# A recurrent layer's scans and factors placed behind its last convolution, and weights prepared three products ahead

## The chip, the cores and the metric

The kernel runs on one core of one Trainium2 chip. A core has five engines that work side by side, each with a queue of its own that it works off in order: TensorE (PE: matrix products, with its weight loads shown as PEld), VectorE (DVE: elementwise work and scans), ScalarE (ACT: functions from tables, copies), GpSimd (POOL: elementwise work, DMA issue) and SyncE (SP: DMA issue). They wait for each other by semaphores. The metric is the device time of one execution in microseconds (us), the median of several runs.

## The reference

A two-layer encoder in float32 on 512 tokens of width 1024. Layer 0 mixes tokens with a stick-breaking attention, layer 1 with a gated linear recurrence; behind each mixer stands an MLP with a squared ReLU (inner width 4096). What matters here, cut:

```python
def rglru_block(h, ...):
    proj = h @ w_in                                   # 1024 -> 2 * 1024
    gate = gelu(proj[..., :1024])
    xc = causal_depthwise_conv(proj[..., 1024:], conv_w, conv_b)    # 4 taps
    r = sigmoid(blocks(xc) @ w_a + b_a)               # 16 blocks of 64 x 64
    i = sigmoid(blocks(xc) @ w_x + b_x)
    log_a = -8 * r * softplus(-lam)
    a = exp(log_a)
    bterm = sqrt(-expm1(2 * log_a)) * (i * xc)
    hs = scan(a, bterm)                               # h[t] = a[t] * h[t-1] + b[t]
    return (hs * gate) @ w_o

def squared_relu_mlp(h, w1, w2):
    u = relu(h @ w1)
    return (u * u) @ w2
```

The last operation is an RMS norm of the sum.

## The kernel before

**Products.** Activations lie with 128 channels on the partitions and the 512 tokens along the row, so 1024 channels are eight blocks, c = 0 to 7. A float32 product is made of three faster ones: each operand is cut into a high half (ScalarE's cast, `wh`, `bh`, `xgh`) and a low half, operand minus high half (VectorE's subtraction, `wl`, `bl`, `xgl`); `three` (L194 to L198) multiplies high by high, high by low, low by high. So each weight slab of 128 x 1024 goes through DMA (L178), a cast (L184) and a subtraction (L191; or on GpSimd, L187 and an accumulating DMA, L188) before TensorE can use it.

**The order of the work.** TensorE's order is the order of the program's text. The other engines' orders are set by a scheduler from priorities and its own estimate of times; `tc.issue_after(x)` makes it place an instruction behind instruction x in the queue. In the recurrent layer `after(x)` is the same.

**The recurrent layer** is a list of steps (L1148). `conv(c)` multiplies a slab of `w_in` (24 products of 128x512), scales by the norm (L1068), makes the convolution from one ScalarE operation (L1075) and three taps on VectorE (L1077), then the high half `bh` (L1083, ScalarE) and the low half `bl` (L1084, VectorE). `gates(c)` multiplies these by the 128x256 gate weights (L1097 to L1099, six products) and takes two sigmoids (L1104, L1105). `rates(chunks)` makes the factors: Tanh (L1113), Exp (L1115), and two VectorE operations (L1117, L1119) with one on GpSimd (L1118). `recur(chunks)` takes Sqrt (L1126), multiplies (L1127) and scans (L1130). `gate(c)` multiplies the other half of `w_in` and keeps it in `z` (L1136); `gated(chunks)` takes Gelu (L1141), multiplies with the scans' result (L1143) and cuts the product into halves (`bh` in L1144, `bl` in L1145), in the same `bh` and `bl` tiles: the operand of the output projection. Change of a function's table on ScalarE is an instruction of its own (ACT_TABLE_LOAD). The blocks go through factors, scans and gating in three groups: 0 to 2, 3 to 5, 6 and 7. Before the change the factors of the second group wait in ScalarE's queue for the high half of convolution 6 (`high` at that time), and its scans in VectorE's for the last tap (`tap`) of convolution 7.

**The output projection** (L1165) runs over the eight columns k of the gated operand, and for each over four output blocks with three products: 96 products, in the banks `ps_o` and `ps_z`.

**The MLP's second product** (`Mlp.down`) makes a quarter of the inner width at a time, as seven products P1 to P7 on sums of blocks instead of eight; each has two halves g. `block` adds two weight blocks (L861, or an accumulating DMA, L854), `operand` cuts them (L839 on ScalarE, L840 on VectorE), `times` multiplies (L873), `collect` adds a bank to the result `c` (L882). In the last quarter an explicit order stands: `prepare` sums and cuts the weights of a product two places ahead of the product. The collects of P2 come behind the cut of the latest prepared weights. In the last MLP, `end` squares, scales and stores the output tokens; `finish` scales two halves of a token block, one of them on VectorE (L1223).

Of the kernel before, what the change touches and what calls it, by code (L numbers as in the profile page):

```python
# [14 lines left out]
ALU = mybir.AluOpType  # L15
# [3 lines left out]
S = 512  # L19
# [28 lines left out]
def hybrid_encoder(  # L48
# [22 lines left out]
    V, A, G, PE = nc.vector, nc.scalar, nc.gpsimd, nc.tensor  # L71
# [195 lines left out]
    with ExitStack() as actx:  # L267
# [18 lines left out]
        for i in range(2):  # L286
            both = []
            for nm in ("h", "l"):
                t = sp.tile([P, 2 * P], F32R, tag=f"last{nm}{i}", name=f"last{nm}{i}")
# [434 lines left out]
    class Mlp:  # L724
# [118 lines left out]
        def block(self, q4, name, g, far):  # L843

            _, b, to, *_ = self.PRODUCTS[name]
            if b == "b21":
                t = wpool.tile([P, C, P], F32, tag="raw", name="raw", bufs=3)
                t = t.rearrange("p (j k) f -> p j (k f)", j=2)
                nc.sync.dma_start(out=t, in_=self.weights(q4, g, b))
                self.raws[b, g] = t  # L850
            raw = self.raws[b, g]
            if name in far:

                G.dma_start(out=raw, in_=self.weights(q4, g, to), accum_op=ALU.add)  # L854
            elif to:

                ahead = None
                if far and (name, g) != ("P5", 0):
                    ahead = self.ready if name == "P5" else self.before
                with tc.issue_after(ahead.ins) if ahead else nullcontext():  # L860
                    V.tensor_tensor(raw, raw, self.raws[to, g], ALU.add)  # L861
            return self.operand(raw)

        def times(self, name, g, i, w, ps, new, cols=slice(0, S)):
# [13 lines left out]
        def collect(self, name, i, ps, cols=slice(0, S)):  # L878
            out, less = self.PRODUCTS[name][4:]
            y = self.c[out][:, i, cols]  # L880
            if (out, i) in self.begun:
                V.tensor_tensor(y, y, ps, ALU.subtract if less else ALU.add)  # L882
            else:
                self.begun.add((out, i))
                A.activation(y, ps, AF.Copy, scale=-1.0 if less else 1.0)

        def down(self, q4, far=(), end=None):
            sums = {}

            def product(name, g, w=None):  # L890
                w = w or self.block(q4, name, g, far)
                to = self.PRODUCTS[name][3]
                new = name in ("P1", "P5", "P2")
                if to not in sums:
                    sums[to] = [self.bank() for _ in range(2)]
                for i in range(2):
                    self.times(name, g, i, w, sums[to][i], new)
                if g:

                    first = end and name == "P2"  # L900
                    with tc.issue_after(self.cut.ins) if first else nullcontext():
                        for i in range(2):
                            self.collect(name, i, sums[to][i])

            if end is None:
                for name in ("P1", "P5", "P6", "P3", "P7", "P2", "P4"):
                    for g in range(2):
                        product(name, g)
                return

            order = [("P1", 0), ("P5", 0), ("P2", 0), ("P1", 1), ("P2", 1), ("P5", 1)]
            order += [(name, g) for name in ("P6", "P3", "P7", "P4") for g in range(2)]
            ws = {}

            def prepare(*at):

                if at != ("P7", 1):
                    self.before = self.cut
                ws[at] = self.block(q4, *at, far)

            for at in order[:2]:
                prepare(*at)
            for at, ahead in zip(order[:-2], order[2:]):
                prepare(*ahead)
                product(*at, ws.pop(at))
            end([ws["P4", g] for g in range(2)], sums["X"])

# [83 lines left out]
    with ExitStack() as rctx:  # L1011
# [25 lines left out]
        def after(act):  # L1037

            return tc.issue_after(act.ins) if act is not None else nullcontext()

        xc, aa, om, z, hs, gin, gw, exps = ({} for _ in range(8))

        TURNS = ["acc", "acc", "t", "t", "o", *("acc", "acc", "t", "t") * 3]
        turns = [0, 0]
# [17 lines left out]

        def conv(c):

            nonlocal begin, tap, high, low
            ps = dense_in(C + c)
            with after(low if c < 3 else None):
                V.tensor_tensor(ps, ps, r, ALU.mult)  # L1068
            aa[c], xc[c], om[c] = (
                rp1.tile([P, S], F32, tag=t, name=t, bufs=n)  # L1070
                for t, n in (("aa", 5), ("bt", 6), ("om", C))
            )
            x0 = xc[c]
            taps = [cw[:, i * C + c : i * C + c + 1] for i in range(4)]
            begin = A.activation(x0, ps, AF.Identity, bias=col("conv_b")[:, c : c + 1], scale=taps[3])  # L1075
            for d in range(1, 4):
                tap = V.scalar_tensor_tensor(  # L1077
                    x0[:, d:], ps[:, : S - d], taps[3 - d], x0[:, d:], ALU.mult, ALU.add
                )

            i = C - 4 + c % 4
            xch, xcl = bh[:, i, :], bl[:, i, :]
            high = A.copy(xch, x0)  # L1083
            low = V.tensor_tensor(xcl, x0, f(xch), ALU.subtract)  # L1084
            gin[c] = xch, xcl
            if c < 3:
                gw[c] = gate_weights(c)
# [20 lines left out]
        def rates(chunks):  # L1108

            for c in chunks:  # L1110
                a0 = rp2.tile([P, S], F32, tag="a0", name="a0")
                with after(sig), after(high if c < 6 else None):
                    ex = A.activation(om[c], aa[c], AF.Tanh, scale=c4[:, c : c + 1])  # L1113
                with after(ex):
                    exps[c] = ex = A.activation(a0, aa[c], AF.Exp, scale=c8[:, c : c + 1])  # L1115
                d = rp2.tile([P, S], F32, tag="d", name="d")
                V.scalar_tensor_tensor(d, a0, 1.0, om[c], ALU.add, ALU.mult)  # L1117
                G.tensor_scalar(aa[c], d, -1.0, 1.0, ALU.mult, ALU.add)  # L1118
                V.scalar_tensor_tensor(xc[c], a0, 1.0, xc[c], ALU.add, ALU.mult)  # L1119

        def recur(chunks):
            nonlocal mark
            ex = exps[chunks[-1]]
            for c in chunks:
                with after(ex):
                    mark = A.activation(om[c], om[c], AF.Sqrt)  # L1126
                V.tensor_tensor(xc[c], xc[c], om[c], ALU.mult)  # L1127

                with after(low if c < 3 else tap if c < 6 else None):
                    V.tensor_tensor_scan(om[c], aa[c], xc[c], 0.0, ALU.mult, ALU.add)  # L1130
                hs[c] = om[c]

# [11 lines left out]
                A.copy(bh[:, c, :], z[c])  # L1144
                V.tensor_tensor(bl[:, c, :], z[c], f(bh[:, c, :]), ALU.subtract)  # L1145

        sig = begin = tap = high = low = None
        for what, c in (  # L1148
            (conv, 0), (conv, 1), (conv, 2), (gate, 0), (gate, 1), (gates, 0), (conv, 3), (gates, 1),
            (gate, 2), (gates, 2), (conv, 4), (gates, 3), (rates, range(3)), (conv, 5),  # L1150
            (recur, range(3)), (gates, 4), (gate, 3), (conv, 6), (gates, 5), (gate, 4),
            (rates, range(3, 6)), (conv, 7), (recur, range(3, 6)), (gates, 6), (gate, 5), (gated, range(6)),
            (gate, 6), (gates, 7), (rates, range(6, C)), (recur, range(6, C)), (gate, 7),
            (gated, range(6, C)),
        ):
            with tc.high_priority() if what is conv else nullcontext():
                what(c)
# [17 lines left out]
    with ExitStack() as mctx:  # L1175
# [35 lines left out]
            y = mlp.y(t, h)[:, cols]  # L1211
            G.tensor_tensor(y, y, gb[:, h * S : (h + 1) * S][:, cols], ALU.mult)

        def finish(t, h, i, cut=None):

            ts = slice(t * P, (t + 1) * P)
            rt = work.tile([P, 1], F32, tag="rt", name="rt")
            A.activation(rt, ss[:, t, i : i + 1], AF.Sqrt, bias=bias[:, t : t + 1], scale=1.0 / D)
            V.reciprocal(rt, rt)
            done, y = mlp.y(t, 1 - h), mlp.y(t, h)  # L1220
            A.activation(done, done, AF.Copy, scale=rt)
            nc.sync.dma_start(out=out[ts, (1 - h) * S : (2 - h) * S], in_=done)
            V.scalar_tensor_tensor(  # L1223
                y[:, cut:], y[:, cut:], rt, gb[:, h * S : (h + 1) * S][:, cut:], ALU.mult, ALU.mult
            )
            if cut:
                V.tensor_scalar(y[:, :cut], y[:, :cut], rt, None, ALU.mult)
            nc.sync.dma_start(out=out[ts, h * S : (h + 1) * S], in_=y)

        def end(ws, xs):  # L1230
            for t in range(2):
                square(t, 0, 0)
                scaled(t, 0)
                square(t, 1, 1, end=True)
                finish(t, 1, 1)
            for t in range(2, 4):
                square(t, 1, 0)
                scaled(t, 1)
# [83 lines left out]
```

## Time and profile before

| | us |
|---|---|
| median of 3 runs | 1083.57 (1082.63 to 1083.65) |
| the profiled execution | 1083.71 |
| its span, first to last instruction | 1082.0 |
| TensorE busy | 1061.5 |
| VectorE busy | 820.7 |
| ScalarE busy | 568.0 |
| GpSimd busy | 169.3 |

A row of a timeline has the start and the duration in us, the engine, the line of the kernel, the operation, output <- input by the program's names and shapes; in brackets the idle time of the engine before it, and what ended that. Equal instructions that follow each other are merged into one row with their count (x2). Consecutive instructions of an engine overlap by some 0.1 us, so a row's end is a little behind the next row's start. PE rows overlap by more: matmuls are pipelined, and their distance counts rather than their duration. A row of windows has a stretch, its length, the busy time and count of each engine, then the granted clock of TensorE as a share of its full speed (PEclk), the DMA share and GB/s.

### The profile page before, as it was taken

The page shows a single profiled execution, that of the slowest core. Times are in us where ns is not written, and L with a number is a line of the kernel's source. Part 1 is how long each engine was busy: PE and PEld are TensorE (multiplying, and loading weights), DVE is VectorE, ACT ScalarE, POOL GpSimd, SP SyncE. Part 2 cuts the span into 40 slices and gives each one's busy share as a digit, 9 for nine tenths or more (in the row PEclk, how much of TensorE's full clock was granted, in tenths as well). Part 3 has the DMA queues.
Part 4 walks back from the last instruction along what each step waited for, and adds up shares of the span by engine and source line. Part 5 has one row for each costly group of instructions (what it writes and reads, how often), then busy time and mean ns, then how long its engine had stood idle before and what let it go on. Part 6 is the DMA issues. An engine that isn't in the chain of part 4 may idle for free.

```text
span 1082.0 us, 13601 instructions
## 1 busy us (share of the span) xinstructions
PE 1061.5 (98%) x4992; PEld 879.0 (81%) x4992; DVE 820.7 (76%) x1073; ACT 568.0 (52%) x826; POOL 169.3 (16%) x199
## 2 busy tenths in 40 slices
PE   8999999999999999999999999899999999999997
PEld 6888888787888888888888777687888888888885
DVE  7788787829897597597687868975696597597776
ACT  6767676726554344344346467944445344344345
POOL 2344444410000000000001654022000000000012
PEclk9999999999999999999999999899999999999999
DMA  7745454526205305305342694242305305305103
GB/s 232 198 118 144 126 145 96 158 75 250 81 27 187 98 20 175 117 18 178 98 83 74 167 221 118 78 159 94 117 20 175 117 12 184 117 5 190 59 13 104
DMA packets 44034, 125.71 MB, mean 116 GB/s; under 512 B 7744, under 2 KB 8512, under 8 KB 43968
## 3 DMA queue, kind: packets, MB, share of 16 engines
q1 hardware_dynamic: 41088, 115.94, 34.3%
q0 software_dynamic: 2304, 8.39, 4.5%
q8 instruction: 39, 0.64, 0.2%
q10 hardware_dynamic: 576, 0.52, 0.2%
q14 instruction: 27, 0.22, 0.1%
HBM read 104.91 MB, written 2.10 MB: 99 GB/s over the span
## 4 chain that ended last, share of the span: by engine, by line
PE 82%; DVE 7%; ACT 5%; DMA 3%; issue 2%; SPq 0%; ACTq 0%; DVEq 0%
PE ps_t L873 9%; PE ps_o L873 6%; PE ps_z L873 6%; PE ps_acc L196 5%; PE ps_acc L197 5%; PE ps_acc L198 5%; PE ps_acc L873 5%; PE ps_o L196 4%; PE ps_o L198 4%; PE ps_o L197 4%; PE ps_z L196 3%; PE ps_z L197 3%; PE ps_t L196 3%; PE ps_z L198 3%; PE ps_t L197 3%; PE ps_t L198 3%
## 5 line engine op out<-in xcount | busy, mean ns | idle before, releaser
L184 ACT CAST wh<-raw 128x1024 fp32r<-128x1024 f32 (+2 forms) x136 | 119.8, 902 | 133.1 <-PE ps_o L198 34.5
L839 ACT CAST wh<-b 128x1024 fp32r<-128x1024 f32 x96 | 100.3, 1050 | 130.8 <-PE ps_o L873 25.0
L191 DVE TENSOR_TENSOR wl<-raw,wh 128x1024 fp32r<-128x1024 f32 (+2 forms) x126 | 132.2, 1065 | 25.8 <-ACT wh L184 25.7
L840 DVE TENSOR_TENSOR wl<-b,wh 128x1024 fp32r<-128x1024 f32 x96 | 116.9, 1222 | 24.3 <-ACT wh L839 24.2
L196 PE MATMUL ps_acc<-xgh,wh 128*128 128x512 f32 x304 | 122.4, 403 | 1.2 <-ACT wh L165 0.8
L197 PE MATMUL ps_acc<-xgh,wl 128*128 128x512 f32 x304 | 119.1, 392 | 0.5 <-DVE wl L166 0.5
L198 PE MATMUL ps_acc<-xgl,wh 128*128 128x512 f32 x304 | 119.0, 392 | 0.1
L854 POOL DMA_DIRECT2D b<-in_w_dn x6 | 5.4, 906 | 638.3 <-DVE wl L840 315.2
L548 DVE TENSOR_TENSOR_SCAN scan<-keep,later 128x128 f32<-128x128 f32 (+1 forms) x64 | 59.3, 927 | 19.8 <-ACT keep L538 15.6
L196 PE MATMUL ps_o<-xgh,wh 128*128 128x512 f32 x176 | 69.5, 395 | 0.2 <-DVE x L700 0.2
L197 PE MATMUL ps_o<-xgh,wl 128*128 128x512 f32 x176 | 68.6, 390 | 0.0
L198 PE MATMUL ps_o<-xgl,wh 128*128 128x512 f32 x176 | 68.6, 390 | 0.0
L198 PEld LDWEIGHTS ps_acc<-xgl,wh 128*128 128x128 f32 x304 | 57.1, 188 | 12.8 <-DVE xgl L116 0.5
L196 PE MATMUL ps_t<-xgh,wh 128*128 128x512 f32 x168 | 67.1, 399 | 0.0
L793 ACT ACTIVATE u<-u 128x512 f32<-128x512 f32 x64 | 39.4, 630 | 52.5 <-DVE u L792 52.5
L196 PEld LDWEIGHTS ps_acc<-xgh,wh 128*128 128x128 f32 x304 | 57.1, 188 | 11.6 <-ACT wh L165 1.0
L197 PE MATMUL ps_t<-xgh,wl 128*128 128x512 f32 x168 | 66.1, 393 | 0.0
L198 PE MATMUL ps_t<-xgl,wh 128*128 128x512 f32 x168 | 66.0, 393 | 0.0
L197 PEld LDWEIGHTS ps_acc<-xgh,wl 128*128 128x128 f32 x304 | 57.3, 188 | 10.5 <-DVE wl L166 1.2
L552 POOL TENSOR_TENSOR w<-w,scan 128x128 f32<-128x128 f32 (+1 forms) x64 | 53.7, 841 | 52.5 <-DVE scan L548 49.8
L861 DVE TENSOR_TENSOR b<-b,b 128x1024 f32<-128x1024 f32 x46 | 56.0, 1219 | 0.2
L803 DVE TENSOR_TENSOR u<-u 128x256 f32<-128x256 f32 x128 | 49.5, 420 | 2.4 <-ACT u L793 1.7
(325 smaller groups left out, 2745.7 us busy)
## 6 DMA issues: line engine op xcount, KB each, us to landing
raw<-in_w_m SPq DMA_DIRECT2D x64, 512.0 KB, 3.6
b<-in_w_dn SPq DMA_DIRECT2D x48, 512.0 KB, 4.2
raw<-in_w_dn SPq DMA_DIRECT2D x16, 512.0 KB, 3.5
raw<-in_w_in SPq DMA_DIRECT2D x16, 512.0 KB, 4.2
raw<-in_w_qk SPq DMA_DIRECT2D x12, 512.0 KB, 3.6
wl<-raw POOLq DMA_DIRECT2D x10, 512.0 KB, 6.0
x<-in_xT SPq DMA_DIRECT2D x16, 256.0 KB, 4.6
raw<-in_w_ro SPq DMA_DIRECT2D x8, 512.0 KB, 3.3
```

The source lines that it names most:

```text
L184: A.copy(wh[:, k, :], raw[:, k, :])
L191: V.tensor_tensor(wl[:, k, :], raw[:, k, :], f(wh[:, k, :]), ALU.subtract)
L196: PE.matmul(ps, wh, ah, start=start, stop=False)
L197: PE.matmul(ps, wl, ah, start=False, stop=False)
L198: PE.matmul(ps, wh, al, start=False, stop=stop)
L548: V.tensor_tensor_scan(sc[:, S - n : S][:, ::-1], keep[:, :n][:, ::-1], later[:, S - n :][:, ::-1], 1.0, ALU.mult, ALU.max,)
L552: G.tensor_tensor(wt, wt, sc[:, S - n + 1 : S + 1], ALU.mult)
L803: V.tensor_tensor(u[:, out, :], u[:, x, :], u[:, y, :], op)
L839: A.copy(wh, raw)
L840: self.cut = V.tensor_tensor(wl, raw, f(wh), ALU.subtract)
L861: V.tensor_tensor(raw, raw, self.raws[to, g], ALU.add)
L873: PE.matmul(ps, x[:, block, ts], y[:, jj, cols], start=first and n == 0, stop=last and n == 2, skip_group_check=not new,)
```

## The change

Four edits:

1. In the list of steps convolution 7 comes ahead of the second group's factors. Those factors now wait in ScalarE's queue for the high half of convolution 7 (a dictionary `highs` keeps each; the first group's still wait for convolution 4's, and the third's for none).
2. The second group's scans wait in VectorE's queue for convolution 7's low half instead of its last tap.
3. In the last quarter of both MLPs weights are prepared three products ahead instead of two. P2's collects come behind the latest sum of blocks (L861) instead of the latest cut, and P5's behind the last cut of P6's weights.
4. In the last MLP the VectorE scaling of the first two token blocks comes behind the latest collect (`mlp.added`).

The order of TensorE's and of SyncE's instructions is unchanged; on the other three queues instructions change places, and none is added or removed.

```diff
         def down(self, q4, far=(), end=None):
...
-                    first = end and name == "P2"
-                    with tc.issue_after(self.cut.ins) if first else nullcontext():
+                    first = {"P2": self.sum, "P5": last_cut.get("P6")}.get(name) if end else None
+                    with tc.issue_after(first.ins) if first else nullcontext():
                         for i in range(2):
                             self.collect(name, i, sums[to][i])
...
                 ws[at] = self.block(q4, *at, far)
-
-            for at in order[:2]:
+                last_cut[at[0]] = self.cut
+
+            for at in order[:3]:
                 prepare(*at)
-            for at, ahead in zip(order[:-2], order[2:]):
-                prepare(*ahead)
+            for at, ahead in zip(order[:-2], (*order[3:], None)):
+                if ahead:
+                    prepare(*ahead)
                 product(*at, ws.pop(at))
...
-            high = A.copy(xch, x0)
+            highs[c] = high = A.copy(xch, x0)
...
-                with after(sig), after(high if c < 6 else None):
+                with after(sig), after(highs.get(chunks[-1] + 2)):
                     ex = A.activation(om[c], aa[c], AF.Tanh, scale=c4[:, c : c + 1])
...
-                with after(low if c < 3 else tap if c < 6 else None):
+                with after(low if c < 6 else None):
                     V.tensor_tensor_scan(om[c], aa[c], xc[c], 0.0, ALU.mult, ALU.add)
...
-            (recur, range(3)), (gates, 4), (gate, 3), (conv, 6), (gates, 5), (gate, 4),
-            (rates, range(3, 6)), (conv, 7), (recur, range(3, 6)), (gates, 6), (gate, 5), (gated, range(6)),
+            (recur, range(3)), (gates, 4), (gate, 3), (conv, 6), (gates, 5), (gate, 4), (conv, 7),
+            (rates, range(3, 6)), (recur, range(3, 6)), (gates, 6), (gate, 5), (gated, range(6)),
...
-            V.scalar_tensor_tensor(
-                y[:, cut:], y[:, cut:], rt, gb[:, h * S : (h + 1) * S][:, cut:], ALU.mult, ALU.mult
-            )
+            with tc.issue_after(last.ins) if last else nullcontext():
+                V.scalar_tensor_tensor(
+                    y[:, cut:], y[:, cut:], rt, gb[:, h * S : (h + 1) * S][:, cut:],
+                    ALU.mult, ALU.mult,
+                )
...
-                finish(t, 1, 1)
+                finish(t, 1, 1, last=mlp.added)
```

More of the change, by code (lines that the diff above doesn't have):

```diff
@@ L860, in block @@
                 with tc.issue_after(ahead.ins) if ahead else nullcontext():
-                    V.tensor_tensor(raw, raw, self.raws[to, g], ALU.add)
+                    self.sum = V.tensor_tensor(raw, raw, self.raws[to, g], ALU.add)
             return self.operand(raw)
@@ L881, in collect @@
             if (out, i) in self.begun:
-                V.tensor_tensor(y, y, ps, ALU.subtract if less else ALU.add)
+                self.added = V.tensor_tensor(y, y, ps, ALU.subtract if less else ALU.add)
             else:
@@ L887, in down @@
         def down(self, q4, far=(), end=None):
-            sums = {}
+            sums, last_cut = {}, {}
             def product(name, g, w=None):
@@ L1039, in after @@
             return tc.issue_after(act.ins) if act is not None else nullcontext()
-        xc, aa, om, z, hs, gin, gw, exps = ({} for _ in range(8))
+        xc, aa, om, z, hs, gin, gw, exps, highs = ({} for _ in range(9))
         TURNS = ["acc", "acc", "t", "t", "o", *("acc", "acc", "t", "t") * 3]
@@ L1063, in conv @@
         def conv(c):
-            nonlocal begin, tap, high, low
+            nonlocal begin, high, low
             ps = dense_in(C + c)
@@ L1076, in conv @@
             for d in range(1, 4):
-                tap = V.scalar_tensor_tensor(
+                V.scalar_tensor_tensor(
                     x0[:, d:], ps[:, : S - d], taps[3 - d], x0[:, d:], ALU.mult, ALU.add
@@ L1145, in gated @@
                 V.tensor_tensor(bl[:, c, :], z[c], f(bh[:, c, :]), ALU.subtract)
-        sig = begin = tap = high = low = None
+        sig = begin = high = low = None
         for what, c in (
@@ L1212, in scaled, with finish @@
             G.tensor_tensor(y, y, gb[:, h * S : (h + 1) * S][:, cols], ALU.mult)
-        def finish(t, h, i, cut=None):
+        def finish(t, h, i, cut=None, last=None):
             ts = slice(t * P, (t + 1) * P)
@@ L1222, in finish @@
             nc.sync.dma_start(out=out[ts, (1 - h) * S : (2 - h) * S], in_=done)
-            V.scalar_tensor_tensor(
-                y[:, cut:], y[:, cut:], rt, gb[:, h * S : (h + 1) * S][:, cut:], ALU.mult, ALU.mult
-            )
+            with tc.issue_after(last.ins) if last else nullcontext():
+                V.scalar_tensor_tensor(
+                    y[:, cut:], y[:, cut:], rt, gb[:, h * S : (h + 1) * S][:, cut:],
+                    ALU.mult, ALU.mult,
+                )
             if cut:
```

## The prediction, made before the result was known

> **What bounds the kernel now.** I read the page first, then TensorE's waits, then the timelines around the longest one.
>
> ```profile
> span 1082.0 us, 13601 instructions
> PE 1061.5 (98%) x4992; PEld 879.0 (81%) x4992; DVE 820.7 (76%) x1073; ACT 568.0 (52%) x826; POOL 169.3 (16%) x199
> ```
>
> TensorE is busy for 98% of the span, so only its own waits and slow stretches can be won or lost. Its waits (engine, tile and line, who was waited for: total us, times, longest):
>
> ```profile
> PE ps_o L1099 <- DVE bl L1084: 4.1, 2, 3.7
> PE ps_t L873 <- DVE c L882: 1.2, 2, 0.9
> PE ps_t L873 <- DVE wl L840: 0.6, 2, 0.4
> ```
>
> The first holds the longest wait: the gate products of channel block 7 wait for the low half of the last convolution. The other two belong to the last quarters of the two MLPs. TensorE's timeline (start, us, instruction, idle time before it):
>
> ```profile
> 671.63 0.39 PE L198 MATMUL ps_t<-xgl,wh 128*128 128x512 f32 x1
> 683.95 0.39 PE L198 MATMUL ps_acc<-xgl,wh 128*128 128x512 f32 x1
> 685.16 0.39 PE L1098 MATMUL ps_o<-bh,gl 128*128 128x512 f32 x1
> 689.21 0.79 PE L1099 MATMUL ps_o<-bl,gh 128*128 128x512 f32 x1 [3.66 <-DVE bl L1084]
> 690.23 0.63 PE L1098 MATMUL ps_o<-bh,gl 128*128 128x512 f32 x1
> 690.65 0.63 PE L1099 MATMUL ps_o<-bl,gh 128*128 128x512 f32 x1
> 697.92 0.40 PE L196 MATMUL ps_o<-bh,wh 128*128 128x512 f32 x1
> 698.39 0.40 PE L198 MATMUL ps_o<-bl,wh 128*128 128x512 f32 x1
> ```
>
> The last convolution's own product ends at 671.63 + 0.39 = 672.02. The gate products stall until 689.21. The rows at 690.23 and 690.65, one step, stand 0.42 us apart, those at 697.92 and 698.39, two steps, 0.47, so 0.23 a step: after the stall TensorE runs at half rate. At 697.92 the out-projection loop begins, with column 0 of the gated output (`bh`, `bl`). The windows show the granted clock (PEclk, the column after the bracketed counts):
>
> ```profile
> 686.50:687.00 0.50, 0.00 (x0) 0.00 (x0) 0.50 (x1) 0.50 (x2) 0.00 (x0) 0.98 0.00 0
> 687.00:687.50 0.50, 0.00 (x0) 0.00 (x0) 0.50 (x2) 0.50 (x2) 0.00 (x0) 0.50 0.00 0
> 693.00:693.50 0.50, 0.50 (x2) 0.40 (x2) 0.50 (x1) 0.50 (x2) 0.00 (x0) 0.50 0.00 0
> 693.50:694.00 0.50, 0.50 (x3) 0.36 (x3) 0.50 (x2) 0.50 (x2) 0.00 (x0) 0.69 0.00 0
> ```
>
> The clock halves at about 687.0, 1.4 us into the idle time, and is whole again at about 693.8, 4.6 us after work resumed; the half-rate phase is 6.8 us long.
>
> **Part 1: the scans behind the last low half.** VectorE's timeline:
>
> ```profile
> 664.71 1.52 DVE L1077 SCALAR_TENSOR_TENSOR bt<-ps_acc,colt,bt 128x511 f32<-128x511 f32 x2
> 666.74 0.74 DVE L1077 SCALAR_TENSOR_TENSOR bt<-ps_acc,colt,bt 128x509 f32<-128x509 f32 x1
> 683.99 3.45 DVE L1130 TENSOR_TENSOR_SCAN om<-aa,bt 128x512 f32<-128x512 f32 x3
> 687.35 1.20 DVE L191 TENSOR_TENSOR wl<-raw,wh 128x1024 fp32r<-128x1024 f32 x1
> 688.47 0.69 DVE L1084 TENSOR_TENSOR bl<-bt,bh 128x512 fp32r<-128x512 f32 x1
> 696.55 0.69 DVE L1117 SCALAR_TENSOR_TENSOR d<-a,om 128x512 f32<-128x512 f32 x1 [0.84 <-ACT a L1115]
> 697.76 1.10 DVE L1145 TENSOR_TENSOR bl<-z,bh 128x512 fp32r<-128x512 f32 x1
> 709.48 1.29 DVE L1145 TENSOR_TENSOR bl<-z,bh 128x512 fp32r<-128x512 f32 x2
> ```
>
> Three scans and a slab's low half (683.99 to 688.5) stand ahead of the low half L1084. In the changed order the whole of convolution 7 comes ahead of the second group's factors on VectorE and ScalarE. From 672.02: ScalarE casts two out-projection slabs first; the second takes the weight buffer that this product frees, so it runs 672.05 to 673.1 (1.05, the cast row below). VectorE then cuts that slab (1.20; the next instruction starts at 674.25), does three taps (1.52 + 0.74, to 676.5); ScalarE's high half runs 676.6 to 677.2, the low half is there at 677.9. TensorE wants it at about 684.6 (683.95 and three steps of 0.23): no wait, 6.7 us to spare. Scans, gated products and the slab's cut together stay off the path here.
>
> **Part 2: the factors behind that convolution.** Here the cost arises, on ScalarE's queue, which is in order. The factors (Tanh, Exp), Sqrt, the sigmoids of gate 6, the six Gelus, the sigmoids of gate 7 and block 6's factors now all stand between 677.1 and the copy of column 0 (`bh`, L1144); before, the factors were done ahead of convolution 7 and the copy stood ahead of gate 7's sigmoids. ScalarE's timeline of before has each piece:
>
> ```profile
> 651.55 1.28 ACT L1126 ACT_TABLE_LOAD   x1
> 656.98 1.05 ACT L184 CAST wh<-raw 128x1024 fp32r<-128x1024 f32 x1
> 667.58 0.62 ACT L1083 CAST bh<-bt 128x512 fp32r<-128x512 f32 x1 [1.94 <-DVE bt L1077]
> 668.10 0.72 ACT L1113 ACTIVATE om<-aa,c 128x512 f32<-128x512 f32 x1
> 674.27 1.28 ACT L1126 ACT_TABLE_LOAD   x1
> 684.80 1.28 ACT L1141 ACT_TABLE_LOAD   x1
> 690.16 0.61 ACT L1144 CAST bh<-z 128x512 fp32r<-128x512 f32 x1
> 690.79 1.28 ACT L1104 ACT_TABLE_LOAD   x1
> 692.67 0.61 ACT L1144 CAST bh<-z 128x512 fp32r<-128x512 f32 x1
> 696.42 2.17 ACT L1144 CAST bh<-z 128x512 fp32r<-128x512 f32 x4
> ```
>
> - Tanh to the Sqrt table: 674.27 - 668.10 = 6.17 (three factors and a slab, as after): 677.1 to 683.3.
> - Table, three Sqrts, table, two sigmoids: 656.98 - 651.55 = 5.43: to 688.7.
> - Table, six Gelus, a slab: 690.16 - 684.80 = 5.36: to 694.1.
> - Table, two sigmoids, Tanh, table, Exp: 696.42 - 690.79 = 5.63, less the copy that stood between (0.5 of 0.61, as instructions overlap): 5.1, to 699.2.
>
> The copy of column 0 runs then, to 699.8. VectorE has two operations of block 6's factors ahead of the low half of column 0 (697.76 - 696.55 = 1.21 after Exp, which ends at 699.3): it starts at 700.55, takes 0.69 and ends at 701.25. So TensorE's third product of the loop starts at 701.3, against 698.39: **+2.9 us**. ScalarE has no idle time in that chain, so it can't shrink by much: without the slab ahead of the taps it would begin 0.7 us earlier (low end +2.2); one contended cut (1.10 for 0.69) and waits between queues make it 0.8 later (+3.7).
>
> TensorE goes through gates and gate 7's product without a stall and reaches the loop at 684.2 + 30 x 0.23 = 691.1, then idles 8.7 us. Nothing covers that. Later columns: one column is 12 x 0.23 = 2.8 us of TensorE, one low half 0.6, so columns 1 to 5 are in time. Columns 6 and 7 were there at 710.8 (709.48 + 1.29) and move by about 4 us to 715, wanted at 720.
>
> **The half rate.** Before it cost 11 products from 689.2 to 693.8 at 0.43 for 0.23: 2.2 us. After the new idle time it recurs. If the 6.8 us phase fell wholly into the idle time it would cost 0; if wholly behind it, 3.4. I take 2.2, the row nearest; it is a new cost only because the old one is already inside 698.39. [...]
>
> **Part 3: MLP, three ahead, and the late scaling.** TensorE in the last quarters:
>
> ```profile
> 564.95 0.49 PE L873 MATMUL ps_t<-wl,sh 128*128 128x512 f32 x1 [0.17 <-DVE wl L840]
> 1054.57 0.39 PE L873 MATMUL ps_t<-wh,sh 128*128 128x512 f32 x1
> 1055.40 0.50 PE L873 MATMUL ps_t<-wl,sh 128*128 128x512 f32 x1 [0.44 <-DVE wl L840]
> 1068.68 0.39 PE L873 MATMUL ps_t<-wh,sl 128*128 128x512 f32 x1
> 1069.93 0.47 PE L873 MATMUL ps_t<-wh,bh 128*128 128x512 f32 x1 [0.86 <-DVE c L882]
> ```
>
> A step is normally 0.23, so 1055.40 costs 0.60 + 0.11 of slow start = 0.7; 564.95 by the same overhead 0.4; 1069.93 costs 1.02 + 0.07 = 1.1. The block sum L861 moves ahead of two collects (1.2 us on VectorE), and its cast ahead of a square on ScalarE, so the weight cut comes about 1.2 us earlier and both first waits end. The final scaling (two operations, 1.7 us) moves behind the `c` collects, so the third ends; it delays no product, and VectorE idles afterwards. Together **-2.2 us**; low end -1.0 if the next cut or collect is late instead. Queues: SP keeps its order; the fetch of the MLP's first slab, which waits for a slab's cut, comes about 3 us later, costed at nothing since the loop's 96 x 0.23 = 22 us of products lie ahead of its use (without them, up to 3 us). On POOL only a scaling moves behind an accumulating DMA, which then starts earlier.
>
> **Sum.** +2.9 + 2.2 - 2.2 = +2.9 us on a span of 1082.0. The profiled execution took 1083.71, the median is 1083.57, 0.14 below it: 1086.4.
>
> **The rivals.**
> - *Faster: column 0 is in time.* One mechanism: ScalarE reaches the copy before TensorE reaches the loop. Then 697.92 becomes 691.1, -6.8, and with the MLPs -2.2: 1074.5. It breaks even with no change if column 0's low half starts TensorE at 698.4, that is 2.9 us less in ScalarE's chain, with half rate as assumed. For: the sum counts on one order of four queues. Against: only 0.7 us of the chain is not ScalarE at work. Chance 0.07.
> - *Same: the half rate falls into the idle time.* 8.7 us of idle is longer than the 6.8 us phase: half-rate cost 0 to 1.3 gives +0.7 to +2.0, 1084.3 to 1085.6. Against: before, the clock rose only after 4.6 us of work. Chance 0.2.
> - *Slower by more: both unknowns bad.* Half rate 3.4, MLP gain 1.0: +5.3, 1088.9; a longer chain adds 0.8. Chance 0.13.
> - *The change doesn't do what it says*, the low half stays late: excluded but for 0.03 by the 6.7 us to spare; then 1081.4 from the MLP part.
>
> **How the numbers follow.** The forecast case (half rate 1.4 to 3.4, MLP -1.5 to -2.2) has 0.57, practically all slower. 0.2% of 1083.57 is 2.2 us, about what a measurement of this kernel tells from none: a forecast of +2.9 stands close above it. Slower 0.57 + 0.13 = 0.70; same 0.20 + 0.02; faster 0.07 + 0.01. The range 1084.0 to 1089.4 takes in the same and the bad case and leaves the faster ones out; the forecast's own is 1085.7 to 1088.4.
>
> **What would show it.** Right: no wait of `ps_o` for `bl` of the convolution over 0.5 us; a new wait of about 8.6 us of `ps_o` for ScalarE's `bh` copy of gated output, and a second, short one for its `bl`; granted clock 0.5 across it; the waits for `c` and `wl` at the quarters' ends down to one of 0.3. Wrong: the loop's third product before 699, no idle time ahead of it, or full clock at resumption.

## The result and the profile after

The changed kernel takes 1089.49 us (median; 1088.46 to 1090.6) against 1083.61 beside it: 1.0056 times the time before, interval 1.0038 to 1.0073. The forecast was 1086.4. A second set of runs (below) gave 1088.51 against 1083.11, ratio 1.0045, interval 1.0031 to 1.0059. The kernel is slower, by 5.4 to 5.9 us. The profiled execution took 1088.46 us with this span and these busy times:

```profile
span 1086.8 us, 13604 instructions
PE 1062.5 (98%) x4992; PEld 880.2 (81%) x4992; DVE 823.7 (76%) x1073; ACT 568.3 (52%) x826; POOL 170.4 (16%) x199
```

The span grew by 1086.8 - 1082.0 = 4.8 us. In code lines of the recurrent layer add two to the numbers of before. TensorE's waits in the recurrent layer:

```profile
PE ps_o L196 <- ACT bh L1146: 8.8, 1, 8.8
PE ps_o L198 <- DVE bl L1147: 0.6, 1, 0.6
PE ps_z L1101 <- DVE bl L1086: 0.4, 1, 0.4
```

The 3.7 us wait of the gate products for the last low half is gone. In its place stands one of 8.8 us, for ScalarE's copy of gated column 0, and a short one for that column's low half on VectorE. TensorE's timeline, with the places that answer to those shown of before:

```profile
683.34 0.40 PE L198 MATMUL ps_acc<-xgl,wh 128*128 128x512 f32 x1
690.35 0.39 PE L198 MATMUL ps_t<-xgl,wh 128*128 128x512 f32 x1
699.56 0.79 PE L196 MATMUL ps_o<-bh,wh 128*128 128x512 f32 x1 [8.83 <-ACT bh L1146]
701.40 0.80 PE L198 MATMUL ps_o<-bl,wh 128*128 128x512 f32 x1 [0.62 <-DVE bl L1147]
706.18 0.39 PE L197 MATMUL ps_o<-bh,wl 128*128 128x512 f32 x1
1059.82 0.39 PE L873 MATMUL ps_t<-wh,sh 128*128 128x512 f32 x1
1060.05 0.39 PE L873 MATMUL ps_t<-wl,sh 128*128 128x512 f32 x1
1068.62 0.50 PE L873 MATMUL ps_t<-wl,bh 128*128 128x512 f32 x1 [0.25 <-DVE wl L840]
1074.48 0.47 PE L873 MATMUL ps_t<-wh,bh 128*128 128x512 f32 x1 [0.35 <-DVE rt L1221]
```

Set against the same products of before, these rows say where the time came from:

| place | before | after | after minus before |
|---|---|---|---|
| last product ahead of `gates(7)` (L198) | 683.95 | 683.34 | -0.6 |
| third product of the out-projection loop | 698.39 | 701.40 | +3.0 |
| a product of the last MLP's last quarter | 1054.57 | 1059.82 | +5.25 |
| the next one, which waited before | 1055.40 | 1060.05 | +4.65 |
| the one that waited for `c` before | 1069.93 | 1074.48 | +4.55 |
| span | 1082.0 | 1086.8 | +4.8 |

So the recurrent layer loses 3.6 us up to the loop's third product and 2.2 more in the loop; the last quarter wins some of it back. The 2.2 is the clock: the eleven steps from the row at 701.40 to the one at 706.18 take 4.78 us, and at 0.23 a step they would take 2.53. Windows (the number after the bracketed counts is the granted clock):

```profile
695.50:696.00 0.50, 0.00 (x0) 0.00 (x0) 0.50 (x1) 0.50 (x2) 0.00 (x0) 0.84 0.00 0
696.00:696.50 0.50, 0.00 (x0) 0.00 (x0) 0.34 (x2) 0.50 (x2) 0.00 (x0) 0.50 0.00 0
699.50:702.70 3.20, 2.52 (x5) 1.62 (x6) 3.20 (x6) 3.20 (x7) 1.00 (x1) 0.50 0.00 0
705.50:706.00 0.50, 0.50 (x3) 0.41 (x2) 0.50 (x1) 0.49 (x2) 0.00 (x0) 0.50 1.06 401
706.00:706.50 0.50, 0.50 (x4) 0.42 (x3) 0.50 (x2) 0.23 (x1) 0.00 (x0) 0.92 0.50 197
```

The clock halves at about 695.8, 5.1 us into the idle time, and is whole again at about 706.1, 6.5 us after work resumed: a phase of 10.2 us, where before it was 6.8. ScalarE's timeline shows the chain that holds the loop up:

```profile
676.07 0.62 ACT L1085 CAST bh<-bt 128x512 fp32r<-128x512 f32 x1 [2.89 <-DVE bt L1079]
676.60 0.72 ACT L1115 ACTIVATE om<-aa,c 128x512 f32<-128x512 f32 x1
682.76 1.28 ACT L1128 ACT_TABLE_LOAD   x1
688.34 1.28 ACT L1143 ACT_TABLE_LOAD   x1
693.81 1.28 ACT L1106 ACT_TABLE_LOAD   x1
698.91 1.64 ACT L1146 CAST bh<-z 128x512 fp32r<-128x512 f32 x3
```

From convolution 7's high half to the copy of column 0 ScalarE works without a break. VectorE's rows at both ends of it:

```profile
676.73 0.69 DVE L1086 TENSOR_TENSOR bl<-bt,bh 128x512 fp32r<-128x512 f32 x1 [0.74 <-ACT bh L1085]
700.25 2.30 DVE L1147 TENSOR_TENSOR bl<-z,bh 128x512 fp32r<-128x512 f32 x3
```

The convolution's low half is there at 677.4, over six microseconds before TensorE asks for it. At the other end the loop waits for the first of three low halves.

### The profile page after: what moved, and what is told of

Its sections match the earlier page's. It is cut to its first block, busy times and chain, and to the rows that moved or that the text cites. A ratio compares the mean times of both kernels' runs of the same rounds, so it can differ in the third digit from the quotient of the medians.

```text
span 1086.8 us, 13604 instructions
## 1 busy us (share of the span) xinstructions
PE 1062.5 (98%) x4992; PEld 880.2 (81%) x4992; DVE 823.7 (76%) x1073; ACT 568.3 (52%) x826; POOL 170.4 (16%) x199
## 4 chain that ended last, share of the span: by engine, by line
PE 80%; DVE 7%; ACT 6%; DMA 4%; issue 2%; SPq 1%; ACTq 0%; DVEq 0%
PE ps_t L873 9%; PE ps_o L873 6%; PE ps_z L873 6%; PE ps_acc L196 5%; PE ps_acc L198 5%; PE ps_acc L197 5%; PE ps_acc L873 4%; PE ps_o L198 4%; PE ps_o L196 4%; PE ps_o L197 4%; PE ps_t L197 3%; PE ps_t L196 3%; PE ps_t L198 3%; PE ps_z L196 3%; PE ps_z L198 3%; PE ps_z L197 3%
## 5 line engine op out<-in xcount | busy, mean ns | idle before, releaser
L198 PE MATMUL ps_acc<-xgl,wh 128*128 128x512 f32 x304 | 119.1, 392 | 0.1
L198 PE MATMUL ps_o<-xgl,wh 128*128 128x512 f32 x176 | 68.6, 390 | 0.0
L198 PEld LDWEIGHTS ps_acc<-xgl,wh 128*128 128x128 f32 x304 | 57.1, 188 | 12.8 <-DVE xgl L116 0.5
L196 PEld LDWEIGHTS ps_acc<-xgh,wh 128*128 128x128 f32 x304 | 57.2, 188 | 10.5 <-ACT wh L165 0.4
L198 PE MATMUL ps_t<-xgl,wh 128*128 128x512 f32 x168 | 65.5, 390 | 0.0
L861 DVE TENSOR_TENSOR b<-b,b 128x1024 f32<-128x1024 f32 x46 | 55.9, 1218 | 0.2
```

Of the source, the lines that this page charges most:

```text
L196: PE.matmul(ps, wh, ah, start=start, stop=False)
L198: PE.matmul(ps, wh, al, start=False, stop=stop)
L861: self.sum = V.tensor_tensor(raw, raw, self.raws[to, g], ALU.add)
```

## The experiments

The theory before them: the time comes from the second group's factors. Their new wait (for convolution 7's high half, L1114) starts ScalarE's chain some 9 us later than before (Tanh at 676.60, before at 668.10, where all the work ahead ran 0.6 us later); the idle time this makes brings a stretch at half clock; and Part 3 wins less than was forecast. The rivals: that Part 1 (the scans moved) costs it, since gated products now stand behind later scans on VectorE; that the half rate is most of it; that the copies stand in the wrong place in an otherwise sufficient chain; and that Part 3 loses somewhere.

**The recurrent part and the MLP part apart.** `e1_recurrent` has the first two edits of the list alone, `e2_mlp` the other two; `e3_scans` only the second, one line:

```diff
-                with after(low if c < 3 else tap if c < 6 else None):
+                with after(low if c < 6 else None):
```

> Edits 1 and 2 alone (recurrent layer), the MLPs as before. Theory A (the loss is ScalarE's queue ahead of column 0 and the half rate behind the idle time, the MLP edits give back only 0.8 us as the two traces show): 6.5 to 7 us slower than before, about 1090.3. Theory B (the prediction's sum held for the recurrent layer, and the MLP edits are to blame for the rest): +5.1, about 1088.7, no more. TensorE idles 8.8 us for the copy of column 0 in both.

> Edits 3 and 4 alone (MLP), the recurrent layer as before. Theory A: 0.3 us won in the first MLP, 0.6 in the last, part of it given back there to a new wait for a cut and one for a reciprocal: -0.8, about 1082.8. The prediction's theory: all three waits end, -2.2, about 1081.4. Theory B (three ahead costs something elsewhere): slower than before, 1084 or more.

> Edit 2 alone: the second group's scans behind the last low half, the order of the steps as before; only a cut and the low half pass three scans on VectorE, ScalarE's order is unchanged. Theory A (moving the scans costs nothing, the factors' move costs all): the gate products wait 0.5 instead of 3.7 us, the half rate there ends, the out-projection loop begins some 3.9 us earlier at column 0's low half (694.5), less 0 to 2.2 if a 2 us wait there halves the clock: -1.5 to -4, 1079.5 to 1082. Theory C (the scans behind the low half delay the gated columns, so moving them is part of the loss): no faster than 1083.

Measured beside the same runs of before (1083.46): 1088.87, ratio 1.005 (1.0038 to 1.0062); 1082.36, ratio 0.9988 (0.998 to 0.9997); and 1079.58, ratio 0.9962 (0.9951 to 0.9974). The recurrent part alone costs 5.4 us. That is Theory B's number, the prediction's own sum of 5.1, and not the 6.5 to 7 of Theory A. The MLP part wins 1.1, between the 0.8 of Theory A and the 2.2 of the prediction; its interval, a gain of 0.3 to 2.2, excludes neither. The two add up to a loss of 4.3, less than the 5.4 to 5.9 of the whole change; the intervals overlap, and the rest is not explained. Moving the scans alone wins 3.9: Part 1 is no cost but the best part of the change, and what is left to edit 1 is 1088.87 - 1079.58 = 9.3 us. A row each of ScalarE and TensorE, and two windows, of the kernel with the scans alone:

```profile
688.98 0.61 ACT L1144 CAST bh<-z 128x512 fp32r<-128x512 f32 x1
```

```profile
693.36 0.50 PE L198 MATMUL ps_o<-bl,wh 128*128 128x512 f32 x1 [0.98 <-DVE bl L1145]
```

```profile
688.00:692.00 4.00, 3.82 (x17) 2.74 (x15) 4.00 (x7) 3.97 (x7) 0.00 (x0) 1.00 0.00 0
692.00:696.00 4.00, 3.02 (x13) 2.17 (x12) 3.15 (x6) 3.98 (x7) 0.00 (x0) 1.00 0.42 131
```

The copy of column 0 runs at 688.98 (698.91 after), the third product at 693.36 (701.40), and the clock stays whole. Edit 1 by itself gives the same order of instructions on every engine as edits 1 and 2, so once the factors stand behind convolution 7, the scans' new wait changes nothing.

Start times of two executions also differ by what ran ahead: here up to 2.6 us. A distance inside one execution is free of that. From the last product ahead of `gates(7)` to the loop's third product it is 14.4 us before, 18.1 after (701.40 - 683.34), 18.1 with edits 1 and 2 alone, and 10.6 with the scans alone. So edit 1 moves the loop by 7.5 us.

**Everything but the factors' place.** `b1_scans_mlp` has edits 2, 3 and 4. Its order on every engine is that of the changed kernel with a single wait put back:

```diff
-                with after(sig), after(highs.get(chunks[-1] + 2)):
+                with after(sig), after(high if c < 6 else None):
```

(with convolution 7 back behind `rates(3 to 5)` in the list, so that `high` is convolution 6's).

> Edits 2, 3 and 4 without edit 1: the scans behind the low half in the old order of steps, and the MLP edits. If the two gains measured alone (-3.9 and -1.1) add: -5.0, 1078.5. If the MLP gain was only scatter: 1079.6.

Measured 1078.93, ratio 0.9959 (0.9946 to 0.9971). ScalarE and TensorE there:

```profile
667.77 0.72 ACT L1115 ACTIVATE om<-aa,c 128x512 f32<-128x512 f32 x1
```

```profile
694.22 0.50 PE L198 MATMUL ps_o<-bl,wh 128*128 128x512 f32 x1 [0.98 <-DVE bl L1147]
```

Tanh begins at 667.77 where it begins at 676.60 in the changed kernel, and the loop's third product comes at 694.22 instead of 701.40. By the ratios the one wait costs 9.3 to 10.5 us (1.0045 or 1.0056, less 0.9959, of 1083). This settles the cause of the loss: the distance to the loop's third product is 10.6 us here and 18.1 in the changed kernel, so 7.5 us of it stand there already; what follows behind it is the half clock of the next run. Beside the scans alone (0.9962) the MLP edits win 0.3 us here, which the intervals can't tell from nothing.

**How much is the clock?** `e4_keep_busy` is the changed kernel with 38 products that nothing reads, ahead of the loop, so that TensorE has no idle time there:

```diff
+        busy = bank("acc")
+        for _ in range(38):
+            PE.matmul(busy, xgh[:, 0, :P], xgh[:, 0, :], start=True, stop=True)
         begun = {}
```

> The changed kernel with 38 more products of 128x512, whose result nobody reads, put into TensorE's 8.8 us of idle time ahead of the out-projection loop (38 x 0.23 = 8.7 us). Nothing else changes. Theory H (the half rate behind the idle time costs 2.2 to 3 us): granted clock 1.00 through the loop, 2 to 3 us faster than the changed kernel, 1086.5 to 1087.5. Rival (the delay of column 0 is all, the clock costs nothing on the path): as the changed kernel, 1089 to 1090.

Measured 1086.11, ratio 1.0026 (1.0015 to 1.0037). The third product and a window behind it:

```profile
700.85 0.50 PE L198 MATMUL ps_o<-bl,wh 128*128 128x512 f32 x1 [1.10 <-DVE bl L1147]
```

```profile
700.00:705.00 5.00, 4.15 (x18) 3.41 (x19) 5.00 (x8) 4.98 (x8) 0.26 (x1) 1.00 0.18 35
```

The clock is whole, and the third product stands where it stood, 18.1 us behind the last product ahead of `gates(7)`: that it starts 0.55 us earlier is what ran ahead. The kernel is 2.1 to 3.2 us faster than the changed one (ratios 1.0045 and 1.0056 against 1.0026). The half rate is thus about a quarter of what the wait costs. The rest is ScalarE's chain, which the added products leave as it is.

**Is it the copies' place in the chain?** `e7_copies_first` holds the sigmoids of gates 6 and 7 back until the six copies of gated columns have run:

```diff
-            with after(mark), after(begin):
+            with after(mark), after(begin), after(copied):
...
-                A.copy(bh[:, c, :], z[c])
+                copied = A.copy(bh[:, c, :], z[c])
```

> The changed kernel, in which the sigmoids of gates 6 and 7 wait for the latest copy of gated output: on ScalarE gate 7's sigmoids and block 6's factors go behind the six copies of columns 0 to 5, all else stays. Theory A (column 0 is late because those pieces, 5.1 us of ScalarE, stand ahead of its copy): the copy of column 0 comes at about 693.7, its low half after the cut of a slab lets TensorE's third product start at about 697 instead of 701.4; 4 to 4.5 us faster than the changed kernel, 1084 to 1086, with the half rate still there. Rival (the place on ScalarE isn't what holds column 0; VectorE's gated products or scans are): 1088 or more.

Measured 1087.37, ratio 1.004 (1.0027 to 1.0054): no gain that these runs can tell from the changed kernel's 1.0045 to 1.0056. The forecast was 1084 to 1086. Its ScalarE, VectorE and TensorE, from an execution that was the longest of its five (1090.65) and ran 2.6 us later already ahead of the chain:

```profile
678.64 0.62 ACT L1085 CAST bh<-bt 128x512 fp32r<-128x512 f32 x1 [2.90 <-DVE bt L1079]
696.27 1.65 ACT L1147 CAST bh<-z 128x512 fp32r<-128x512 f32 x3
701.74 0.69 ACT L1106 ACTIVATE aa<-ps_o,colt 128x512 f32<-128x512 f32 x1
```

```profile
698.73 1.89 DVE L1148 TENSOR_TENSOR bl<-z,bh 128x512 fp32r<-128x512 f32 x3
```

```profile
702.48 0.79 PE L196 MATMUL ps_o<-bh,wh 128*128 128x512 f32 x1 [9.19 <-ACT aa L1106]
703.50 0.63 PE L198 MATMUL ps_o<-bl,wh 128*128 128x512 f32 x1
```

Counted from convolution 7's high half the copies come 17.6 us on, 5.2 earlier than in the changed kernel (22.8), and the loop's first product waits all the same, now 9.19 us for the sigmoid of `gates(7)` at 701.74. That sigmoid reads the bank `ps_o` which the loop's first output takes over. The third product is 17.6 us behind the last one ahead of `gates(7)`, for 18.1: the new order wins 0.5 us there. Both things that the loop needs, the copy and the bank, hang on the end of the same chain, so this change of its order wins next to nothing, and its earlier start (`b1_scans_mlp`) wins 7.5.

**Why Part 3 won so little.** `e8_mlp3` has edit 3 alone, without the late scaling (edit 4):

> Edit 3 alone (three ahead and the collects' places), without the late scaling, the recurrent layer as before. Theory A (VectorE's queue has no free time at the end of the last quarter, so the late scaling adds nothing): as edits 3 and 4 together, -1.1, about 1082.4. The prediction's theory (the late scaling ends a wait of its own, 1.1 us): 1 us slower than both edits, 1083.4.

Measured 1082.9, ratio 0.9993 (0.9981 to 1.0004): half way between the two forecasts, 1082.4 and 1083.4, so the time decides nothing. The traces do. Every kernel has one cut of weights in the last quarter that comes after a short wait for ScalarE (at 1047.78 here, 1047.41 in `e2_mlp`, 1049.38 before). From it to the end of the span it is 31.9 us here, 32.1 to 32.3 in the seven traces with both edits, and 32.6 to 32.7 in the four without either. The late scaling adds nothing, and the last quarter wins about 0.5 us. `b3_scans_low` is the best version below without edits 3 and 4, and prices the pair where no stretch at half clock blurs it (mean granted clock 0.999, against 0.994 in the changed kernel):

> Part 1 and column 0's low half ahead of the gated products of columns 2 to 5, without Parts 2 and 3: beside the version with Part 3 (1078.06) it gives what Part 3 is worth in a kernel whose recurrent loop no longer meets the half rate. By the trace's shift of the MLP blocks (0.3 in the first, 0.5 in the second) it is 0.8: 1078.9. By the run of Part 3 alone (1082.36 against 1083.4) 1.1: 1079.2. By the prediction's own term, 2.2: 1080.3.

Measured 1079.19, ratio 0.9964 (0.9951 to 0.9977), against 0.9951 with them: 1.1 us by the medians, 1.4 by the ratios, and the intervals overlap. `m1_no_sums` tests the reason. It is that best version without the two block sums of the seventh product's weights:

```diff
-            elif to:
+            elif to and not (far and name == "P7"):
```

The product then takes unsummed weights, so the output is another one.

> The version with Parts 1 and 3 and column 0's low half first (1078.06), with the two sums of the seventh product's weights in the last quarter left out (VectorE's two of 128x1024, 2.35 us together; the product then takes the unsummed weights). If Part 3 lost its gain because VectorE has no idle time in the last quarter, the two waits of TensorE that stand there now (0.2 for the low half of weights, 0.4 for a collect behind the second reciprocal) end or shrink, and it is 0.4 to 0.7 shorter: 1077.5. The rival, that the reciprocal itself comes late from ScalarE's chain of squares and root: the 0.4 stays, the 0.2 goes, 1077.9, and VectorE shows idle time ahead of the reciprocal.

Measured 1077.34, ratio 0.9951 (0.9938 to 0.9964), against 1078.06 and the same ratio, 0.9951, with the sums. Both waits of TensorE end, as the theory says. The same product of the last quarter, first with the sums, then without:

```profile
1063.03 0.47 PE L873 MATMUL ps_t<-wh,bh 128*128 128x512 f32 x1 [0.36 <-DVE rt L1222]
```

```profile
1062.25 0.39 PE L873 MATMUL ps_t<-wh,bh 128*128 128x512 f32 x1
```

It comes 0.78 us earlier, and yet both spans are 1075.5. (Ahead of the sums the second execution was 0.3 us behind, so the product gains 1.1 and the end 0.3.) VectorE shows where the gain stays, again with the sums and without:

```profile
1063.46 2.45 DVE L1227 SCALAR_TENSOR_TENSOR c<-c,rt,gb 128x512 f32<-128x512 f32 x2
1065.83 1.27 DVE L882 TENSOR_TENSOR c<-c,ps_t 128x512 f32<-128x512 f32 x2
```

```profile
1063.05 3.11 DVE L1227 SCALAR_TENSOR_TENSOR c<-c,rt,gb 128x512 f32<-128x512 f32 x2
1066.09 1.27 DVE L882 TENSOR_TENSOR c<-c,ps_t 128x512 f32<-128x512 f32 x2
```

The two moved scalings take 3.11 instead of 2.45, and the collects behind them start at 1066.09 instead of 1065.83. So the theory holds for the waits, and its gain of 0.4 to 0.7 is not told from nothing: behind the last wait VectorE's queue sets the end, not TensorE. That GpSimd's multiplication, which starts at 1062.61 here and at 1063.80 there, is what stretched the scalings was not tried.

**Column 0's low half first.** In `b1_scans_mlp` the loop still waits 0.98 us for column 0's low half. `b2_low_first` puts it ahead of the gated products of columns 2 to 5 on VectorE:

```diff
+            lows = {}
             for c in chunks:
...
-                with after(low):
+                with after(low), after(lows.get(0) if c > 1 else None):
                     V.tensor_tensor(z[c], hs[c], z[c], ALU.mult)
                 A.copy(bh[:, c, :], z[c])
-                V.tensor_tensor(bl[:, c, :], z[c], f(bh[:, c, :]), ALU.subtract)
+                lows[c] = V.tensor_tensor(bl[:, c, :], z[c], f(bh[:, c, :]), ALU.subtract)
```

> The same, and on VectorE the low half of column 0 (with a slab's cut) ahead of the gated products of columns 2 to 5. With edit 2 alone TensorE still waits 1.0 us for that low half at the loop's third product (693.36); here it should be there at about 691.5: 1 to 1.2 us faster than without, 1077.4. If columns 2 to 5 then come late instead: no faster, 1078.5 or more.

Measured 1078.06, ratio 0.9951 (0.9937 to 0.9964). The wait is gone: the third product comes 9.5 us behind the last one ahead of `gates(7)`, 1.1 sooner. This is the fastest version that does all the work, 0.5% below the kernel before and about 1% below the changed one; its interval overlaps that of `b1_scans_mlp`.

**The scatter.** The profiled execution of the changed kernel was its shortest, so `a1_again` ran it once more. If the stretch at half clock sets the scatter, the longer executions show the lower granted clock; if the scatter comes from elsewhere, the clock does not follow the time. Both give the same median:

> The changed kernel once more, unaltered, on the chip and beside the runs of the two kernels below. Its profiled execution (1088.46) was the shortest of its four, the median 1.0 above it. [...] Median 1088.5 to 1089.8 by both.

Measured 1088.51 (1086.74 to 1088.65), ratio 1.0045. The clock does not follow the time: the executions at 1086.74 and at 1088.65 both had 0.994. So the stretch at half clock isn't shown to set the scatter; where it comes from stays open.

## Why the prediction was right or wrong

The direction and the mechanism of the recurrent layer were right, the term of the MLPs was wrong, and the sum was about half of what came: +2.9 forecast, +4.8 in the profiled execution and +5.4 to +5.9 by the medians. The step that failed is Part 3, "Together -2.2 us": the traces show -0.8 and the run of the two MLP edits -1.1. Term by term:

| step | forecast | measured in the trace |
|---|---|---|
| Part 1: low half there, no wait | 677.9 | 677.4, no wait over 0.4 |
| Part 2: third product of the loop | 701.3 (+2.9) | 701.40 (+3.0; +3.6 from the place ahead of it) |
| The half rate | +2.2 (0 to 3.4) | +2.2 (5.25 - 3.0); 2.1 to 3.2 by the runs |
| Part 3 | -2.2 (low end -1.0) | -0.8; -1.1 by the run |

**Part 1** held, and the run of that edit alone adds what the prediction didn't price: without Part 2 it is a win of 3.9 us. Its first rival, column 0 in time, was near: with the scans alone only 1 us of waiting is left (693.36), and with the low half first none. Part 2's chain alone excluded it.

**Part 2** held piece by piece: Tanh to the Sqrt table 6.17 forecast and 682.76 - 676.60 = 6.16 measured; to the Gelu table 5.43 and 5.58; to the table of `gates(7)` 5.36 and 5.47; to the copy 5.1 and 5.10. The wait was forecast at about 8.6 us and is 8.83. Two things moved against each other. The chain started 0.5 earlier than forecast (676.60 for 677.1), as all that lies ahead runs 0.6 earlier; and column 0's low half took 1.1 us instead of 0.69, the contended cut that had been kept for the high end:

```profile
L1147 DVE TENSOR_TENSOR bl<-z,bh x3: 678/679/1097, 700.2 to 701.9; 128x512 fp32r<-128x512 f32 x3
```

(durations of the three, least, median and greatest, in ns). Beside it GpSimd ran its step of block 6, `aa`:

```profile
699.81 1.00 POOL L1120 TENSOR_SCALAR aa<-d 128x512 f32<-128x512 f32 x1 [14.28 <-DVE d L1119]
```

It ends at 700.81, and 0.59 later TensorE starts the third product. The low half of 1.10 at 697.76 before ran beside the same step of GpSimd:

```profile
697.32 1.00 POOL L1118 TENSOR_SCALAR aa<-d 128x512 f32<-128x512 f32 x1 [20.30 <-DVE d L1117]
```

In `e7_copies_first` GpSimd's step comes only after these three low halves (VectorE starts the `d` that it reads at 705.67), and they take 1.89 us instead of 2.30. That points to the neighbour on GpSimd; by what means it would stretch the cut is not shown.

**The half rate** came out at the number taken, by luck and not by the reason. The prediction carried the phase's length of before, 6.8 us, into its rival that the half rate falls into the idle time. The phase after is 10.2 us long: it began 5.1 us into the idle time and went on through a stretch (699.5 to 702.7, granted clock 0.50) in which TensorE was busy for 2.52 of 3.20 us. Before, it began after 1.4 us of idle time. What sets its start and its length these two traces don't show.

**Part 3** is the term that failed. All three waits ended, for 0.3 in the first MLP (564.95 before, 564.74 after, in spite of a start 0.1 later), 0.6 at 1055.40 and 0.5 at 1069.93, 1.4 together for the 2.2 forecast. Then two new ones took back part: one of 0.25 for a weight cut (+0.4 by the distance of the products), and one of 0.35 for a reciprocal, which is why the third gain is 0.5 and not 1.1; the end comes another 0.2 later. The step in it that was wrong is "it delays no product, and VectorE idles afterwards". VectorE before and after, at the place from which the scaling was taken and where it went:

```profile
1067.42 1.77 DVE L1223 SCALAR_TENSOR_TENSOR c<-c,rt,gb 128x512 f32<-128x512 f32 x2
1072.94 0.69 DVE L882 TENSOR_TENSOR c<-c,ps_t 128x512 f32<-128x512 f32 x1 [1.96 <-PE ps_t L873]
```

```profile
1071.96 1.72 DVE L840 TENSOR_TENSOR wl<-b,wh 128x1024 fp32r<-128x1024 f32 x1
1074.26 0.15 DVE L1221 RECIPROCAL rt<-rt 128x1 f32<-128x1 f32 x1
1074.92 2.45 DVE L1226 SCALAR_TENSOR_TENSOR c<-c,rt,gb 128x512 f32<-128x512 f32 x2
1077.29 1.27 DVE L882 TENSOR_TENSOR c<-c,ps_t 128x512 f32<-128x512 f32 x2
```

The 1.96 us of idle time that the scaling was to go into are gone: three products' weights ahead, cuts, sums and collects fill VectorE without a break up to the collects at 1077.29, the last cut takes 1.72 for 1.2, and the scaling takes 2.45 for 1.77. The 2.2 was three waits added up as if VectorE had room for whatever comes behind them.

A part of that room was lost to a move that the prediction priced at nothing: "On POOL only a scaling moves behind an accumulating DMA". GpSimd and VectorE before, then after:

```profile
1052.12 1.99 POOL L1212 TENSOR_TENSOR c<-c,gb 128x512 f32<-128x512 f32 x1 [0.20 <-ACT junk L1201]
1054.12 3.50 DVE L840 TENSOR_TENSOR wl<-b,wh 128x1024 fp32r<-128x1024 f32 x3
```

```profile
1060.74 2.15 POOL L1214 TENSOR_TENSOR c<-c,gb 128x512 f32<-128x512 f32 x1
1060.52 3.45 DVE L840 TENSOR_TENSOR wl<-b,wh 128x1024 fp32r<-128x1024 f32 x2
```

Before, the scaling ended as the cuts began, and three cuts took 3.50; after, it runs beside them, and two take 3.45. That is 1.1 us more of VectorE's time. All nine traces with edit 3 show these two cuts at 3.45 or 3.46, and the four without it show three at 3.50. No run has edit 3 with the scaling in its old place, so how much of the 2.2 this cost stays open.

Of the difference between forecast and trace, +2.9 and +4.8, Part 3 is 1.4 and Part 2 counted from the place ahead of it 0.7; against them stands about 0.3 us that the work ahead of the last convolution ran earlier, which no edit explains. The medians lie another 0.6 to 1.1 above the difference of the two profiled executions.

## What to carry to other kernels

When work is moved behind a later event on an in-order queue, follow that queue to its next consumer: here a wait that seemed to tidy ScalarE's order started a 22 us chain without slack 9 us later, and both the operand and the bank that the next loop needed lay at its end. Price each edit of a bundle alone before the bundle; one edit of this change is worth -3.9 us and another +9.3 or more. A wait that ends on the busiest engine is a gain only up to the next queue that is full, so look at the idle time of the engine that is given the moved work after the change, not before it, and at what then runs beside it. Compare distances inside an execution, not start times of two.

## What was not expected of the hardware

The stretch at half clock (granted clock 0.50) had 6.8 us in one kernel and 10.2 in the other, began 1.4 us into the idle time in one and 5.1 in the other, and outlasted a stretch in which TensorE was busy for 2.52 of 3.20 us. With the scans alone, where TensorE's longest wait in this part of the layer is 0.98 us, and with the 38 filling products, where it is 1.10, the granted clock was 1.00 in the windows there. Its price was 2.2 us both times. These are two traces, and no run looked for the limits.
